# Norms of a hybrid encoder trunk: last squares added on VectorE, sums in one set of matmuls, roots spread by transposes, outputs scaled from PSUM

## Chip, cores and metric

The kernel runs on one core of one Trainium2 chip. The metric is the device time of one execution in microseconds. Before the change the median of three runs is 1268.73 us (1267.92 to 1269.37).

## What is computed

The trunk has two residual layers with a token mixer each (a gated spatial MLP, then RWKV-7) and a gated convolutional feed-forward after each mixer. Every one of the four sub-layers is preceded by an RMS norm, and one norm closes the trunk. The sequence is 512 tokens, the model width 1024, all data float32.

```
def rms_norm(x, g):
    y = xf * lax.rsqrt(jnp.mean(xf * xf, axis=-1, keepdims=True) + RMS_EPS)
    return y * g

h = x
for i in range(DEPTH):                       # DEPTH = 2
    hn = rms_norm(h, norm_mix_g[i])
    h = h + (sgu_mixer if i % 2 == 0 else rwkv7_mixer)(hn, ...)
    h = h + conv_ffn(rms_norm(h, norm_ffn_g[i]), ...)
return rms_norm(h, norm_final_g)
```

## The kernel before

The residual stream `h` is held transposed in SBUF: eight tiles of 128 features by 512 tokens. The stages run in the order gating (`sgu`), feed-forward 0 (`ffn`), RWKV (`rwkv_first`, `rwkv_main`), feed-forward 1, output. Matrix products are made from two parts for each operand, a rounded one and the rest (`split`, L224; `mm3`, L316), so that each fp32 product is three matmuls of a fast type. Weights arrive by DMA, ScalarE casts the high part (L236) and VectorE subtracts to get the low part (L237).

**How a norm is made.** Because the norm's factor is one number for each token, the projections run on `h` times the gain without it, and the factor is applied to their results. When a stage updates tile `k` of `h`, `absorb` (L332) makes the operands of the next projection and squares the tile on ScalarE (L342, L345). GpSimd adds the squares of tiles 0 to 6 into `ss` (L347); those of tile 7 stay apart in `sq`. `rstd` (L349) then

- sums over the 128 features on TensorE: for each of four blocks of 128 tokens one matmul of `ss` and one of `sq` against a column of ones (L355, L356), accumulated in a PSUM column. These are plain fp32 matmuls, outside `mm3`;
- takes the inverse roots: VectorE scales and adds epsilon (L372), GpSimd raises to the power -0.5 (L373). This gives a 128x4 tile with tokens on the partitions;
- spreads the roots to all partitions: for each block a matmul whose stationary operand is the root column broadcast to 128x128 and whose moving operand is the identity (L362), into PSUM tile `z`;
- copies `z` to SBUF as `rb` on ScalarE (L365). Consumers multiply by `rb`.

`rstd` is a generator with two steps, so that callers put projections between sums and spread: one projection in a feed-forward (L533 to L539), the second half of the value projection in the gating stage (L456, L472), and in `rwkv_first` parts of two low-rank projections (L678 to L684): four of the eight tiles of the first ahead of the sums, the other four and two tiles of the second between sums and spread, the rest after.

**The output.** `output` (L584) makes the final norm for one half of the tokens. The last projection of feed-forward 1 is cut into token halves and its pieces are ordered by hand (L561), so that the first half's norm runs while TensorE works on the second half. After a half's last piece VectorE adds it to `h` (L569) and ScalarE squares it (L595). ScalarE has multiplied `h` by the gains into four tiles `o` of two features blocks each (L602). Sums (L606, L607), roots, spread (L613) and the copy to SBUF (L616) follow. The scaling by the spread roots is done tile by tile, 128x256 each: six on VectorE and the pair `k == 4` on GpSimd (L622). SyncE stores each pair (L623). In the second half `wait` (L588) puts matmuls without use into TensorE's order ahead of the sums and ahead of the spread (L591).

The order of instructions on each engine comes from a scheduler at compile time; `issue_after` pins a part of it. Each engine then works through its own list in order, and semaphores hold it where an input isn't there yet.

Of the kernel before, what the change touches and what calls it, by code (L numbers as in the profile page):

```python
# [12 lines left out]
F32 = mybir.dt.float32  # L13
F32R = mybir.dt.float32r
AF = mybir.ActivationFunctionType
ALU = mybir.AluOpType
# [4 lines left out]
P = 128  # L21
# [123 lines left out]
class Emit:  # L145
# [203 lines left out]
    def rstd(self):  # L349

        nc = self.nc
        q = self.acc()
        for b in range(4):
            bs = slice(b * P, (b + 1) * P)
            nc.tensor.matmul(q[:, b:b + 1], self.ss[:, bs], self.c("one", 1), start=True, stop=False)  # L355
            nc.tensor.matmul(q[:, b:b + 1], self.sq[:, bs], self.c("one", 1), start=False, stop=True)  # L356
# [4 lines left out]
        for b in range(4):  # L361
            nc.tensor.matmul(z[:, b * P:(b + 1) * P], r[:, b:b + 1].to_broadcast([P, P]), self.c("ident", P),  # L362
                             start=True, stop=True)
# [48 lines left out]
    def sgu(self, gain):  # L412
        nc, tc, A = self.nc, self.tc, self.A
        with ExitStack() as ctx:
# [24 lines left out]
            for hf in range(2):  # L439
# [15 lines left out]
                if hf == 0:  # L455
                    norm = self.rstd()  # L456
                    r = next(norm)
# [126 lines left out]
    def output(self, hs):  # L584
# [8 lines left out]
        n = T // 2  # L593
        sq = self.gp.tile([P, n], F32, tag="sq", bufs=2, name=self.uid("sq"))
        nc.scalar.activation(sq, self.h[KT - 1][:, hs], AF.Square)  # L595
        yield
        q = self.acc()
# [5 lines left out]
        wait(T)  # L603
        for b in range(2):
            bs = slice(b * P, (b + 1) * P)
            nc.tensor.matmul(q[:, b:b + 1], self.ss[:, hs][:, bs], self.c("one", 1), start=True, stop=False)  # L606
            nc.tensor.matmul(q[:, b:b + 1], sq[:, bs], self.c("one", 1), start=False, stop=True)  # L607
# [4 lines left out]
        for b in range(2):  # L612
            nc.tensor.matmul(z[:, b * P:(b + 1) * P], r[:, b:b + 1].to_broadcast([P, P]), self.c("ident", P),  # L613
                             start=True, stop=True)
        rb = self.gp.tile([P, T], F32, tag="rb", bufs=1, name=self.uid("rb"))[:, 0:n]
        nc.scalar.copy(rb, z)  # L616
        yield
        out = self.out.rearrange("k p t -> p k t")
        for k in (0, 2, 4, 6):
            t = o[k // 2]  # L620
            for i in range(2):
                (nc.gpsimd if k == 4 else nc.vector).tensor_tensor(t[:, i], t[:, i], rb, ALU.mult)  # L622
            nc.sync.dma_start(out[:, k:k + 2, hs], t)  # L623
# [42 lines left out]
    def rwkv_first(self, r, ep):  # L666
# [11 lines left out]
        self.dense(lw[0], self.first, hx[:4], last=False)  # L678
        norm = self.rstd()
        next(norm)  # L680
        self.dense(lw[0], self.first, hx[4:], first=False, c0=4 * P)
        self.dense(lw[1], w, hx[:2], last=False)
# [725 lines left out]
```

## Time and profile before

| | us |
|---|---|
| median of three runs | 1268.73 |
| lowest, highest | 1267.92, 1269.37 |
| the profiled execution's own time | 1264.91 |
| its span in the profile | 1263.1 |
| TensorE busy in it | 1241.9 |
| VectorE, ScalarE, GpSimd busy | 856.1, 629.7, 98.0 |

In the profile, PE is TensorE, PEld its weight loads, DVE VectorE, ACT ScalarE, POOL GpSimd, SP SyncE. A timeline row gives the start in the span, the duration (of a merged group if it ends in x2 or more), the engine, the line, the operation and what it writes and reads; brackets give the engine's idle time just before and what ended it. TensorE's matmuls overlap, so its pace is read from one start to the next, not from the duration. A row of the windows view gives for each engine the busy time and the number of instructions, then TensorE's granted clock as a share of full speed, the DMA engines' share and the bytes moved in GB/s. In the chain of waits a row gives the start, the length and the work on the path that ended last.

### The profile page before, as it was taken

The page shows a single profiled execution, that of the slowest core. Times are in us where ns is not written, and L with a number is a line of the kernel's source. Part 1 is how long each engine was busy: PE and PEld are TensorE (multiplying, and loading weights), DVE is VectorE, ACT ScalarE, POOL GpSimd, SP SyncE. Part 2 cuts the span into 40 slices and gives each one's busy share as a digit, 9 for nine tenths or more (in the row PEclk, how much of TensorE's full clock was granted, in tenths as well). Part 3 has the DMA queues.
Part 4 walks back from the last instruction along what each step waited for, and adds up shares of the span by engine and source line. Part 5 has one row for each costly group of instructions (what it writes and reads, how often), then busy time and mean ns, then how long its engine had stood idle before and what let it go on. Part 6 is the DMA issues. An engine that isn't in the chain of part 4 may idle for free.

```text
span 1263.1 us, 19531 instructions
## 1 busy us (share of the span) xinstructions
PE 1241.9 (98%) x7591; PEld 1007.9 (80%) x7591; DVE 856.1 (68%) x1403; ACT 629.7 (50%) x1082; POOL 98.0 (8%) x121
## 2 busy tenths in 40 slices
PE   9999999999999999999999999899999999999997
PEld 6878888888888888877777776678888888888886
DVE  6466568888886454675789897765677777773233
ACT  6544446556555433475676657423544544443322
POOL 4100200000000010000000022222000000000002
PEclk9999999999999999999999999999999999999998
DMA  7332357777656765325868799764222333333332
GB/s 258 104 100 84 130 167 240 247 252 245 195 166 203 228 215 184 97 91 192 218 200 226 215 244 230 213 171 138 96 95 91 99 100 100 96 88 105 92 92 80
DMA packets 115452, 201.65 MB, mean 160 GB/s; under 512 B 21600, under 2 KB 53600, under 8 KB 115360
## 3 DMA queue, kind: packets, MB, share of 16 engines
q10 hardware_dynamic: 39104, 112.87, 29.3%
q1 hardware_dynamic: 76256, 87.54, 23.2%
q8 instruction: 59, 0.97, 0.3%
q14 instruction: 33, 0.27, 0.1%
HBM read 152.93 MB, written 47.45 MB: 159 GB/s over the span
## 4 chain that ended last, share of the span: by engine, by line
PE 86%; DVE 6%; DMA 1%; issue 1%; ACT 1%; POOL 0%; SPq 0%; DVEq 0%; ACTq 0%; POOLq 0%
PE mm L320 9%; PE mm L322 9%; PE mm L321 9%; PE aux L320 6%; PE aux L322 6%; PE aux L321 6%; PE e L321 6%; PE e L320 6%; PE e L322 6%; PE us L321 5%; PE us L322 5%; PE us L320 5%; PE aux L938 1%; DVE tt L1015 1%; DVE pr L1014 1%; PE aux L952 1%
## 5 line engine op out<-in xcount | busy, mean ns | idle before, releaser
L236 ACT CAST w<-w 128x512 fp32r<-128x512 f32 x340 | 206.5, 611 | 360.8 <-PE e L322 91.1
L237 DVE TENSOR_TENSOR w<-w,w 128x512 fp32r<-128x512 f32 x340 | 232.1, 685 | 184.7 <-ACT w L236 184.4
L320 PE MATMUL mm<-mxh,w 128*128 128x512 f32 x416 | 169.7, 408 | 0.2 <-ACT vt L837 0.2
L321 PE MATMUL mm<-mxl,w 128*128 128x512 f32 x416 | 163.8, 394 | 0.0
L322 PE MATMUL mm<-mxh,w 128*128 128x512 f32 x416 | 163.7, 394 | 0.0
L347 POOL TENSOR_TENSOR ss<-ss,sq 128x512 f32<-128x512 f32 x30 | 40.7, 1355 | 770.7 <-issue 592.9
L320 PEld LDWEIGHTS mm<-mxh,w 128*128 128x128 f32 x416 | 78.1, 188 | 20.1 <-issue 3.3
L322 PEld LDWEIGHTS mm<-mxh,w 128*128 128x128 f32 x416 | 78.2, 188 | 16.7 <-issue 0.7
L321 PEld LDWEIGHTS mm<-mxl,w 128*128 128x128 f32 x416 | 78.2, 188 | 15.5 <-issue 1.3
L545 ACT ACTIVATE cv<-z,par 128x512 f32<-128x512 f32 x88 | 71.7, 817 | 29.4 <-DVE z L543 24.4
L322 PE MATMUL aux<-mxh,w 128*128 128x512 f32 x216 | 84.2, 390 | 0.3 <-DVE w L237 0.3
L320 PE MATMUL aux<-mxh,w 128*128 128x512 f32 x216 | 84.5, 391 | 0.0
L320 PE MATMUL us<-mxh,w 128*128 128x512 f32 x216 | 84.5, 391 | 0.0
L321 PE MATMUL aux<-mxl,w 128*128 128x512 f32 x216 | 84.1, 389 | 0.0
L321 PE MATMUL us<-mxl,w 128*128 128x512 f32 x216 | 84.1, 389 | 0.0
L322 PE MATMUL us<-mxh,w 128*128 128x512 f32 x216 | 84.0, 389 | 0.0
L320 PE MATMUL e<-mxh,w 128*128 128x512 f32 x208 | 81.4, 391 | 0.1
L321 PE MATMUL e<-mxl,w 128*128 128x512 f32 x208 | 81.1, 390 | 0.1
L322 PE MATMUL e<-mxh,w 128*128 128x512 f32 x208 | 80.9, 389 | 0.0
L546 DVE SCALAR_TENSOR_TENSOR cv<-z,par,cv 128x512 f32<-128x512 f32 x88 | 66.1, 752 | 19.9 <-ACT cv L545 19.9
L547 DVE SCALAR_TENSOR_TENSOR cv<-z,par,cv 128x512 f32<-128x512 f32 x88 | 66.0, 752 | 2.9
L322 PEld LDWEIGHTS aux<-mxh,w 128*128 128x128 f32 x216 | 40.5, 188 | 9.2 <-DVE w L237 0.8
(1089 smaller groups left out, 2574.8 us busy)
## 6 DMA issues: line engine op xcount, KB each, us to landing
w<-in_wup ACTq DMA_DIRECT2D x88, 512.0 KB, 3.6
w<-in_wdn ACTq DMA_DIRECT2D x32, 512.0 KB, 3.7
st<-std SPq DMA_DIRECT2D x30, 320.0 KB, 6.2
w<-wkd ACTq DMA_DIRECT2D x16, 512.0 KB, 4.9
w<-wvd ACTq DMA_DIRECT2D x16, 512.0 KB, 5.6
w<-wod ACTq DMA_DIRECT2D x16, 512.0 KB, 4.2
w<-in_wdn ACTq DMA_DIRECT2D x16, 384.0 KB, 3.4
w<-in_wsu ACTq DMA_DIRECT2D x8, 512.0 KB, 3.7
```

The source lines that it names most:

```text
L236: nc.scalar.copy(hi[r, :n], src)
L237: (lo_eng or nc.vector).tensor_tensor(lo[r, :n], src, hi[r, :n].bitcast(F32), ALU.subtract)
L320: mm(acc, wh, xh, start=first, stop=False)
L321: mm(acc, wh, xl, start=False, stop=False)
L322: mm(acc, wl, xh, start=False, stop=last)
L347: nc.gpsimd.tensor_tensor(self.ss, self.ss, self.sq, ALU.add)
L545: nc.scalar.activation(c, z[:, 2:], AF.Identity, scale=cw(2, i), bias=self.p("conv_b", l * 44 + i))
L546: nc.vector.scalar_tensor_tensor(c, z[:, 1:T + 1], cw(1, i), c, ALU.mult, ALU.add)
L547: nc.vector.scalar_tensor_tensor(c, z[:, 0:T], cw(0, i), c, ALU.mult, ALU.add)
L938: nc.tensor.matmul(qs[hd][:, c - ch.start, :], bk[H[hd], c, C * hd:C * hd + P], ar[H[hd], c, :], start=True, stop=True)
L952: nc.tensor.matmul(qs[hd][:, c, :], bk[H[hd], c, C * hd:C * hd + P], dg[H[hd], c, :], start=True, stop=True)
L1014: V.tensor_tensor(q, a, b, ALU.mult)
```

## The change

In `rstd` VectorE adds the last tile's squares to the others' sum, and the sums are one matmul for each block instead of two; the gating stage asks for the old form (`whole=False`). Roots are spread by TensorE transposes of the broadcast column in place of matmuls with the identity. In `output` the first half uses the added form; the second keeps both sources, with the matmuls of `ss` for both blocks put ahead of those of `sq`, and the first useless matmul, now 256 columns wide, between them. The spread roots are no longer copied to SBUF: VectorE multiplies each pair of tiles, 128x2x256, by the PSUM tile broadcast over the pair, and GpSimd takes no part. In `rwkv_first` six tiles of the first low-rank projection stand ahead of the sums, and one tile of the second before the spread.

```diff
+    def spread(self, z, r):
+        for b in range(r.shape[-1]):
+            self.nc.tensor.transpose(z[:, b * P:(b + 1) * P], r[:, b:b + 1].to_broadcast([P, P]), self.c("ident", P))
+
-    def rstd(self):
+    def rstd(self, whole=True):
         nc = self.nc
         q = self.acc()
+        if whole:
+            nc.vector.tensor_tensor(self.ss, self.ss, self.sq, ALU.add)
         for b in range(4):
-            bs = slice(b * P, (b + 1) * P)
-            nc.tensor.matmul(q[:, b:b + 1], self.ss[:, bs], self.c("one", 1), start=True, stop=False)
-            nc.tensor.matmul(q[:, b:b + 1], self.sq[:, bs], self.c("one", 1), start=False, stop=True)
+            for i, x in enumerate((self.ss,) if whole else (self.ss, self.sq)):
+                nc.tensor.matmul(q[:, b:b + 1], x[:, b * P:(b + 1) * P], self.c("one", 1), start=i == 0, stop=i == 1 or whole)
...
-        for b in range(4):
-            nc.tensor.matmul(z[:, b * P:(b + 1) * P], r[:, b:b + 1].to_broadcast([P, P]), self.c("ident", P),
-                             start=True, stop=True)
+        self.spread(z, r)
...
-                    norm = self.rstd()
+                    norm = self.rstd(whole=False)
...
+        whole = hs.start == 0
...
-        wait(T)
-        for b in range(2):
-            bs = slice(b * P, (b + 1) * P)
-            nc.tensor.matmul(q[:, b:b + 1], self.ss[:, hs][:, bs], self.c("one", 1), start=True, stop=False)
-            nc.tensor.matmul(q[:, b:b + 1], sq[:, bs], self.c("one", 1), start=False, stop=True)
+        ss = self.ss[:, hs]
+        q = self.acc()
+        if whole:
+            nc.vector.tensor_tensor(ss, ss, sq, ALU.add)
+            for b in range(2):
+                nc.tensor.matmul(q[:, b:b + 1], ss[:, b * P:(b + 1) * P], self.c("one", 1), start=True, stop=True)
+        else:
+            for x in (ss, sq):
+                for b in range(2):
+                    nc.tensor.matmul(q[:, b:b + 1], x[:, b * P:(b + 1) * P], self.c("one", 1), start=x is ss and b == 0,
+                                     stop=x is sq, skip_group_check=True)
+                if x is ss:
+                    wait(n)
...
-        for b in range(2):
-            nc.tensor.matmul(z[:, b * P:(b + 1) * P], r[:, b:b + 1].to_broadcast([P, P]), self.c("ident", P),
-                             start=True, stop=True)
-        rb = self.gp.tile([P, T], F32, tag="rb", bufs=1, name=self.uid("rb"))[:, 0:n]
-        nc.scalar.copy(rb, z)
+        self.spread(z, r)
...
-        for k in (0, 2, 4, 6):
+        for k in range(0, KT, 2):
             t = o[k // 2]
-            for i in range(2):
-                (nc.gpsimd if k == 4 else nc.vector).tensor_tensor(t[:, i], t[:, i], rb, ALU.mult)
+            nc.vector.tensor_tensor(t, t, z.unsqueeze(1).to_broadcast([P, 2, n]), ALU.mult)
             nc.sync.dma_start(out[:, k:k + 2, hs], t)
...
-        self.dense(lw[0], self.first, hx[:4], last=False)
+        self.dense(lw[0], self.first, hx[:6], last=False)
         norm = self.rstd()
         next(norm)
-        self.dense(lw[0], self.first, hx[4:], first=False, c0=4 * P)
-        self.dense(lw[1], w, hx[:2], last=False)
+        self.dense(lw[0], self.first, hx[6:], first=False, c0=6 * P)
+        self.dense(lw[1], w, hx[:1], last=False)
         rb = next(norm)
-        self.dense(lw[1], w, hx[2:], first=False, c0=2 * P)
+        self.dense(lw[1], w, hx[1:], first=False, c0=P)
```

1 line of the change is left out of this document (removed).

## Prediction

> **What bounds the kernel now.** I read the page first, then TensorE's timeline around each norm, the other engines' timelines beside it, and last the chain of waits and fine windows at the end.
>
> ```profile
> span 1263.1 us, 19531 instructions
> ...
> PE 1241.9 (98%) x7591; PEld 1007.9 (80%) x7591; DVE 856.1 (68%) x1403; ACT 629.7 (50%) x1082; POOL 98.0 (8%) x121
> ...
> PE 86%; DVE 6%; DMA 1%; issue 1%; ACT 1%; POOL 0%; SPq 0%; DVEq 0%; ACTq 0%; POOLq 0%
> ```
>
> TensorE is busy for 98% of the span and makes up 86% of the chain that ended last. One long window, the second feed-forward stage, shows how that holds locally:
>
> ```profile
> 905.00:1230.00 325.00, 325.00 (x1435) 269.12 (x1434) 206.16 (x301) 140.99 (x221) 6.45 (x5) 1.00 0.31 96
> ```
>
> All 325.00 us are TensorE's, at a granted clock of 1.00. A pass that TensorE no longer has to make in such a stage should therefore shorten the kernel by its own length. What remains to be seen is whether each norm lies in such a place. Here is the norm of that stage on TensorE:
>
> ```profile
> 891.83 0.28 PE L355 MATMUL us<-cst,ss 128*128 128x1 f32 x2
> ...
> 893.53 0.48 PE L320 MATMUL mm<-mxh,w 128*128 128x512 f32 x1
> ...
> 899.06 1.05 PE L362 MATMUL aux<-cst,rt 128*128 128x128 f32 x8
> 899.87 0.48 PE L320 MATMUL e<-mxh,w 128*128 128x512 f32 x1
> ```
>
> From 891.83 to 893.53 TensorE does the sums: four blocks, two sources, two passes for each fp32 matmul ("x2" in a row), 16 passes in 1.70 us, 0.106 us each. The 24 projection matmuls up to 899.06 take 5.53 us, 0.23 us each. The spread of the roots is 8 passes in 0.81 us, 0.10 each. Nothing in between waits.
>
> **The change, part by part.** *Sums.* In the norms of both feed-forward stages and of the RWKV stage the sums fall from 16 passes to 8: 8 x 0.106 = 0.85 us each, 2.55 us for three. The gating stage keeps both sources there and gains nothing on this part.
>
> VectorE's new add is 128x512 f32; the nearest row is 0.69 us (L543, below). Is it hidden?
>
> ```profile
> 889.15 0.62 ACT L345 ACTIVATE sq<-h 128x512 f32<-128x512 f32 x1
> 892.02 0.62 ACT L236 CAST w<-w 128x512 fp32r<-128x512 f32 x1 [1.75 <-PE e L322]
> 159.24 0.16 DVE L372 TENSOR_SCALAR rs<-aux 128x4 f32<-128x4 f32 x1 [2.65 <-PE aux L356]
> 518.28 0.16 DVE L372 TENSOR_SCALAR rs<-mm 128x4 f32<-128x4 f32 x1 [2.07 <-PE mm L356]
> 893.70 0.16 DVE L372 TENSOR_SCALAR rs<-us 128x4 f32<-128x4 f32 x1 [2.70 <-PE us L356]
> ```
>
> The bracket is VectorE's idle time ahead of the scale step: 2.65, 2.07 and 2.70 us. In the last case it is free from 891.00, the squares are there at 889.77, so the add ends near 891.7, just before the sums at 891.83. The projection matmuls cover it; without that cover it costs 0.7 us a norm. I take nothing.
>
> *Spread.* Four matmuls of two passes become four transposes. The kernel has transposes of the same shape in its scan:
>
> ```profile
> L1260 PE MATMUL aux<-cst,y x32: 271/273/329, 756.3 to 861.3; 128*128 128x128 f32 x32
> ...
> 756.30 0.66 PE L1260 MATMUL aux<-cst,y 128*128 128x128 f32 x4
> 756.71 0.48 PE L320 MATMUL mm<-mxh,w 128*128 128x512 f32 x1
> ```
>
> Eight calls of four make 32, so a transpose is one pass, and four of them take 0.41 us against 0.81. That is 0.40 us in each of four norms (gating, both feed-forwards, RWKV): 1.60 us.
>
> *The moved work in the RWKV stage.* Six matmuls move ahead of the sums, and the spread comes after nine instead of eighteen. No DMA moves with them.
>
> ```profile
> 516.40 0.28 PE L355 MATMUL mm<-cst,ss 128*128 128x1 f32 x2
> ...
> 518.10 0.48 PE L320 MATMUL e<-mxh,w 128*128 128x512 f32 x1
> ...
> 522.27 1.05 PE L362 MATMUL aux<-cst,rt 128*128 128x128 f32 x8
> ...
> 527.05 0.39 PE L322 MATMUL us<-mxh,w 128*128 128x512 f32 x1
> 527.50 0.50 PE L320 MATMUL e<-mxh,w 128*128 128x512 f32 x1
> ...
> 528.30 0.40 PE L320 MATMUL aux<-mxh,w 128*128 128x512 f32 x1
> 528.77 0.51 PE L321 MATMUL e<-mxl,w 128*128 128x512 f32 x1
> ...
> 518.52 1.40 POOL L373 TENSOR_TENSOR rt<-rs,mhalf 128x4 f32<-128x4 f32 x1 [3.40 <-DVE rs L372]
> ...
> 20.87 3.21 POOL L373 TENSOR_TENSOR rt<-rs,mhalf 128x4 f32<-128x4 f32 x1 [2.56 <-DVE rs L372]
> ```
>
> The roots are done at 519.92, 1.82 us after TensorE left the sums at 518.10. Nine matmuls cover 9 x 0.23 = 2.07, so the spread should still find them ready, with 0.25 us to spare. If GpSimd took 3.21 us, as it did in the first norm, TensorE would wait 1.6 us. The spread comes 0.68 us earlier in TensorE's order (three matmuls fewer in all ahead of it) and 0.85 us earlier for the shorter sums, so the spread factor is there about 1.9 us sooner. After the projections TensorE waits for the mixing chain that starts from this factor: 0.22 us over the pitch at 527.50 and 0.24 at 528.77. Bounds are nothing and both; a chain 1.9 us earlier against projections 1.25 us earlier leaves 0.65 for 0.46, so I take 0.45.
>
> *The end.* The output goes in halves of 256 columns. In the first half TensorE still works on the last projection:
>
> ```profile
> 1245.42 0.28 PE L606 MATMUL aux<-cst,ss 128*128 128x1 f32 x2
> ...
> 1246.22 0.36 PE L320 MATMUL mm<-hid12h,w 128*128 128x256 f32 x1
> ...
> 1247.40 0.71 PE L613 MATMUL e<-cst,rt 128*128 128x128 f32 x4 [0.46 <-POOL rt L373]
> ...
> 1250.94 0.28 PE L322 MATMUL mm<-hid21h,w 128*128 128x256 f32 x1
> ...
> 1251.66 0.41 DVE L569 TENSOR_TENSOR h<-h,mm 128x256 f32<-128x256 f32 x1
> ...
> 1248.55 3.19 DVE o L622 x6
> ```
>
> Eight passes become four (0.80 to 0.40) and four spread passes become two (0.10 each, so 0.20): TensorE ends 0.60 us earlier. The wait for the roots (0.46) I leave as it is; the new add (0.41 by the L569 row) could lengthen the first half by that, or the emptier chain could take the wait away. The residual add L569 starts at 1251.66 although the last matmul ended at 1251.22: it is queued on VectorE behind the six scalings of the first half, which run to 1251.74. Four scalings that start some 0.8 us earlier and need 2.5 to 2.8 us end before it is due. That gives 0.40.
>
> ```profile
> 1255.38 0.38 ACT rb L616
> 1255.78 0.42 DVE o L622
> ...
> 1255.83 1.82 POOL L622 TENSOR_TENSOR o<-o,rb 128x256 f32<-128x256 f32 x2 [1.33 <-ACT rb L616]
> ...
> 1257.68 0.37 SPq L623 DMA_DIRECT2D out_yT<-o  x1
> ...
> SPq L623 <- POOL o L622: 57.3, 2, 52.1
> ...
> 1255.00:1255.50 0.50, 0.27 (x3) 0.07 (x1) 0.00 (x0) 0.12 (x1) 0.00 (x0) 0.98 0.00 0
> ...
> 1258.50:1259.00 0.50, 0.00 (x0) 0.00 (x0) 0.44 (x2) 0.00 (x0) 0.00 (x0) 0.50 0.81 262
> 1261.50:1262.00 0.50, 0.00 (x0) 0.00 (x0) 0.00 (x0) 0.00 (x0) 0.00 (x0) 0.50 0.31 105
> ...
> 166.30 0.69 DVE L543 TENSOR_TENSOR z<-mm,rb 128x512 f32<-128x512 f32 x1 [0.17 <-ACT rb L365]
> ```
>
> In the second half two passes less stand between the last squares and the roots (0.22), two less in the spread (0.20), and the copy to SBUF goes (1255.38 to 1255.78, 0.40). Then comes the part that a count of operations would miss: the first store is issued only at 1257.68, 1.90 us after scaling begins, because SyncE's queue has GpSimd's pair first (it ends at 1257.65). From there on the stores bind: bytes flow from about 1258.6 to 1261.65, four times 256 KB in 3.05 us. Without GpSimd the first pair is ready 0.69 us after scaling begins (L543: a 128x512 product with one PSUM operand), and the store goes out at about 0.74. The other pairs follow every 0.7 us, while one store's bytes take 0.76, so the transfer stays the limit and the end moves by 1.90 - 0.74 = 1.16. If the queue still waited for the last pair, the first store would go out 2.8 us after the start and 0.9 would be lost instead.
>
> A rule of the Trainium skill bears on the removed copy: "VectorE: DVE Perf Modes", Rules for kernel authors, says to take the slower PSUM source as it is, or to copy to SBUF first if many operations read it. By the rows of this case the copy costs 0.40 us, and a 128x512 product from PSUM takes 0.69 us where two 128x256 ones from SBUF take 0.42 each, so four readers are not many here. Following the rule's second half would give back the 0.40.
>
> The sum: 2.55 + 1.60 + 0.45 + 0.60 + 0.40 + 0.22 + 0.20 + 0.40 + 1.16 = 7.6 us. The profiled execution took 1264.91 us (span 1263.1), so it would take 1257.3; the median of the three runs, 1268.73, lies 3.8 us higher, and 1268.7 - 7.6 gives 1261.1.
>
> **The rivals.** *The norm's own chain comes late* (0.14). The add or the roots are queued badly and TensorE waits. If the add stands behind the next weight split, whose cast (892.02) ends at 892.64, split and add end at 894.0 and the sums start 2.2 us late. One such norm leaves 5.4 us: 1263.3. So does the slow GpSimd case, with 1262.7. Three norms would leave 1.0, no change. VectorE's long idle times speak against it.
>
> *The early savings are absorbed* (0.08). In the scan TensorE isn't the only limit. If what the gating, first feed-forward and RWKV norms bring (0.40 + 1.25 + 1.25 + 0.45 = 3.35 us) ended in waits there, 4.2 us would remain: 1264.5. Against it: those waits are for work that starts earlier too.
>
> *The transposes are no single pass* (0.05). Then 1.60 and about 0.4 at the end are lost: 1263.1. The 32 rows of L1260 speak against it.
>
> *The clock falls* (0.05), the case in which it gets slower. The column after the engines in the fine windows is the granted clock: it leaves 1.00 in the window 1255.00 to 1255.50, in which TensorE's last passes lie, and is 0.50 for the 7.5 us that are left. So the clock follows recent work, and the change takes counted passes out of five places. A stretch as long as that one at half clock in the middle costs 3.75 us. Two of them eat the gain, and from three on it is slower: 1272.4 with three. Against it, L1260's transposes run among matmuls with the clock at full. "TensorE: Matmul & The Clock Gate", Part 4, of the Trainium skill says that transposes don't count as work for the clock gate; the scan's transposes show no fall, and each new group lasts only 0.4 us among dense matmuls.
>
> **How the numbers follow.** The forecast has 0.68. A measurement of this kernel can tell about 0.2% (2.5 us) from no change. Faster by more: 0.68, with 0.10 of the late chain, 0.06 of the absorbed savings and 0.05 of the transposes, 0.89. The rest of those, 0.06, is within it, and 0.05 is slower. The low end takes the whole wait for roots in the output (0.46) and the spread of the runs (0.8) on top, with further waits in the mixing chain: 1258.8. The high end, 1265.0, takes in the transposes, the absorbed savings and one or two late norms.
>
> **What would show it.** Right: eight passes of 0.85 us in three norms, spreads of 0.41 us, no gap near 526 us, the residual add within 0.4 us of the last matmul, the first store within 0.8 us of the first scaling, and 3.05 us of bytes after it. Wrong: TensorE idle before the sums or before a transpose, a VectorE add queued behind a weight split, stores still in another order than the scalings, or a clock below 1.00 ahead of the end.

## The result and the profile after

The kernel after took 1258.41 us (median of four executions, 1257.85 to 1258.64), the kernel before 1269.05 us beside it (four, 1267.92 to 1271.46): a ratio of 0.9919, interval 0.9897 to 0.9941. The gain is 10.6 us where the prediction summed 7.6, and 1258.4 lies 0.4 us below the predicted range. The profiled execution after took 1258.64 us. From its page:

```profile
span 1256.8 us, 19427 instructions
...
PE 1238.0 (98%) x7543; PEld 1003.2 (80%) x7543; DVE 856.3 (68%) x1403; ACT 627.7 (50%) x1080; POOL 95.0 (8%) x117
...
PE 86%; DVE 7%; issue 1%; POOL 1%; ACT 0%; DMA 0%; DVEq 0%; POOLq 0%; ACTq 0%
```

TensorE still bounds the kernel with 98% of the span. But the two profiled spans differ by 1263.1 - 1256.8 = 6.3 us only, so most of the distance between 6.3 and 10.6 is not in these two traces. First the places of the change. The second feed-forward norm on TensorE's timeline:

```profile
889.77 0.95 PE L362 MATMUL us<-cst,ss 128*128 128x1 f32 x8
890.58 0.48 PE L320 MATMUL mm<-mxh,w 128*128 128x512 f32 x1
...
896.11 0.60 PE L352 MATMUL aux<-cst,rt 128*128 128x128 f32 x4
896.47 0.48 PE L320 MATMUL e<-mxh,w 128*128 128x512 f32 x1
```

The sums take 0.81 us (1.70 before), the spread 0.36 us (0.81). VectorE's new add is done 1.2 us before the sums begin:

```profile
887.90 0.69 DVE L359 TENSOR_TENSOR ss<-ss,sq 128x512 f32<-128x512 f32 x1
```

In the gating stage the shorter spread buys almost nothing. TensorE's waits between 53 and 157 us for the v tiles, before and after (engine, tile and line, what it waited for: us in total, times, longest):

```profile
PE e L495 <- DVE vt L469: 0.2, 1, 0.2
```

```profile
PE e L499 <- DVE vt L473: 0.6, 1, 0.6
```

VectorE's four products of the v tiles depend on the roots, not on the spread; they end when they ended, and TensorE waits for the last of them by what it saved. In the RWKV stage the roots cause no wait, but the pause after the projections stays (0.37 us between the last projection matmul at 523.51 and the first mixing matmul, a pitch being 0.23):

```profile
518.51 0.60 PE L352 MATMUL aux<-cst,rt 128*128 128x128 f32 x4
518.87 0.48 PE L320 MATMUL us<-mxh,w 128*128 128x512 f32 x1
...
523.88 0.50 PE L320 MATMUL e<-mxh,w 128*128 128x512 f32 x1
...
525.10 0.50 PE L321 MATMUL e<-mxl,w 128*128 128x512 f32 x1
```

The end: TensorE's timeline, then VectorE's, then SyncE's first store of the second half, then what SyncE's queue waited for.

```profile
1242.29 0.61 PE L612 MATMUL aux<-cst,ss 128*128 128x1 f32 x4
...
1243.93 0.43 PE L352 MATMUL e<-cst,rt 128*128 128x128 f32 x2 [0.45 <-POOL rt L377]
...
1247.20 0.28 PE L322 MATMUL mm<-hid21h,w 128*128 128x256 f32 x1
```

```profile
1247.52 0.42 DVE L573 TENSOR_TENSOR h<-h,mm 128x256 f32<-128x256 f32 x1 [0.63 <-PE mm L322]
...
1250.67 2.48 DVE L629 TENSOR_TENSOR o<-o,e 128x512 f32<-128x512 f32 x4 [1.36 <-PE e L352]
```

```profile
1251.39 0.37 SPq L630 DMA_DIRECT2D out_yT<-o  x1
```

```profile
SPq L630 <- DVE o L629: 414.9, 4, 410.6
```

The residual add now follows its matmul (VectorE was free for 0.63 us before it). The first store goes out 0.72 us after the first scaling, against 1.90, and SyncE's queue waits for VectorE, no longer for GpSimd. Before the first half's sums TensorE stands still for 0.28 us: the last matmul started at 1241.89, a pitch is 0.12, the sums start at 1242.29, because the add ends at 1242.23.

A landmark is the start of the same instruction in both traces. The gains between landmarks, before minus after:

| from, to | gain there, us |
|---|---|
| start to the gating stage's spread (weights and first loads, nothing changed) | 0.76 |
| gating spread, with its later wait | 0.07 |
| first feed-forward: sums 0.89, spread 0.46 | 1.35 |
| RWKV: sums, spread, move, to the first mixing matmul | 1.44 |
| from there to the second feed-forward sums (nothing changed) | -1.56 |
| second feed-forward: sums 0.89, spread 0.45 | 1.34 |
| output: TensorE 0.33, residual add 0.40, chain to the first scaling 0.97, stores 1.15 | 2.85 |

That makes 6.3 us; the change's own places alone make 7.1. The -1.56 comes from a stretch that the change doesn't touch, shown here by windows of the kernel after (from, to and length, busy us of PE, PEld, DVE, ACT and POOL with their counts, then the granted clock, DMA share, GB/s):

```profile
680.00:681.00 1.00, 1.00 (x8) 0.80 (x7) 1.00 (x4) 0.88 (x2) 0.00 (x0) 1.00 0.28 98
681.00:682.00 1.00, 1.00 (x4) 0.79 (x3) 1.00 (x2) 0.41 (x2) 0.00 (x0) 0.59 0.22 47
...
683.00:684.00 1.00, 1.00 (x6) 0.91 (x5) 0.96 (x5) 1.00 (x3) 0.00 (x0) 0.50 1.04 323
684.00:685.00 1.00, 1.00 (x7) 1.00 (x7) 1.00 (x4) 0.06 (x1) 0.00 (x0) 0.71 0.86 261
685.00:686.00 1.00, 1.00 (x11) 0.59 (x10) 0.91 (x2) 0.97 (x3) 0.00 (x0) 1.00 0.01 2
```

For 3.4 us the clock is 0.50 in the middle of the kernel, and matmuls start every 0.43 us instead of every 0.23. TensorE is "busy" all the while: only the clock's column shows it. The profiled execution before has no such stretch ahead of its end.

### The profile page after: what moved, and what is told of

Its sections match the earlier page's. It is cut to its first block, busy times and chain, and to the rows that moved or that the text cites. A ratio compares the mean times of both kernels' runs of the same rounds, so it can differ in the third digit from the quotient of the medians.

```text
span 1256.8 us, 19427 instructions
## 1 busy us (share of the span) xinstructions
PE 1238.0 (98%) x7543; PEld 1003.2 (80%) x7543; DVE 856.3 (68%) x1403; ACT 627.7 (50%) x1080; POOL 95.0 (8%) x117
## 4 chain that ended last, share of the span: by engine, by line
PE 86%; DVE 7%; issue 1%; POOL 1%; ACT 0%; DMA 0%; DVEq 0%; POOLq 0%; ACTq 0%
PE mm L320 9%; PE mm L322 9%; PE mm L321 9%; PE aux L320 6%; PE aux L322 6%; PE aux L321 6%; PE e L320 6%; PE e L321 6%; PE us L320 6%; PE e L322 6%; PE us L322 6%; PE us L321 6%; DVE tt L1022 1%; PE aux L945 1%; DVE pr L1021 1%
## 5 line engine op out<-in xcount | busy, mean ns | idle before, releaser
L237 DVE TENSOR_TENSOR pwl<-pw,pwh 128x512 fp32r<-128x512 f32 (+1 forms) x51 | 34.8, 682 | 19.8 <-DMA wkd<-pwl 4.6
```

The costliest lines, as they stand in the source:

```text
L237: (lo_eng or nc.vector).tensor_tensor(lo[r, :n], src, hi[r, :n].bitcast(F32), ALU.subtract)
```

## The experiments

Two theories. *A, the clock:* the parts are worth about what the prediction summed, and the rest of the gain is half-clock stretches that differ from execution to execution and cost the kernel before more. *B, a part worth more:* some part brings more than was priced. Later a third question came up, what the moved matmuls do. Parts are judged by landmarks in the traces, times by all executions with their mean clock.

**Both kernels again, and each half of the change** (e1 before; e2 after with the output function of before, here its core; e3 before with the output function of after; e4 after).

```
-            nc.vector.tensor_tensor(t, t, z.unsqueeze(1).to_broadcast([P, 2, n]), ALU.mult)
+            for i in range(2):
+                (nc.gpsimd if k == 4 else nc.vector).tensor_tensor(t[:, i], t[:, i], rb, ALU.mult)
```

> The kernel before, unchanged, to see where its executions differ from each other: its profiled one took 1264.91 us, its timed ones 1267.92 to 1271.46. Theory A (clock): the slower ones hold one or more stretches of about 3.4 us at half the granted clock in the scan, worth up to 1.7 us each, as the changed kernel's trace shows one at 681 to 684.5; then this trace, if it lies near 1268 or above, shows two or more windows with a granted clock of 0.50 ahead of the end, and the time above 1264.9 is about 1.7 us for each. Theory B (memory): the clock is 1.00 throughout and the extra 3 to 6 us lie in waits for DMA in the RWKV stage. Ratio 1.000 in either case.

> Everything of the change but the output: sums, transposes and the moved matmuls in the norms ahead of the four sub-layers; the output as before. By the landmarks of the two traces this part brings 0.46 in each of four spreads, 0.89 in each of three sums, less about 0.5 lost to a different order in the gating stage: 4.0 us, ratio 0.9968. If the excess of the measured gain (10.6) over that of the traces (6.3) belongs to the norms, it brings 7 to 8 us, ratio 0.994.

> Only the output changed, the norms as before. By the two traces' landmarks (the first half's last matmul 3.41 us earlier, the span's end 6.3 us earlier) this part brings 2.9 us, ratio 0.9977; by the prediction's terms 3.0. If the excess belongs to the output it brings 6 to 7 us, ratio 0.995. The first store is issued within 0.8 us of the first scaling and bytes flow for 3.05 us after it.

> The changed kernel, unchanged, beside the others on one chip: ratio 0.992. Theory A: the number of half-clock stretches ahead of the end differs from execution to execution and with it the time, 1.6 us for one. Theory B: no such stretch, the same time within 0.5 us. If norms and output are independent its gain is the sum of the two parts' gains within 1 us.

e1: 1268.91 us (1266.40 to 1274.14, 12 executions). e2: 1262.10 (1258.77 to 1264.38, 6). e3: 1266.40 (1261.68 to 1269.42, 12). e4: 1257.69 (1257.14 to 1258.60, 5). Ratios: 1.0006 [0.9992, 1.0021], 0.9947 [0.9930, 0.9964], 0.9979 [0.9964, 0.9993], 0.9917 [0.9903, 0.9930]. By medians the norms bring 6.8 us, more than their landmarks (4.2 us in the table above), the output 2.5 (2.9). The two together make 9.3, 1.9 less than the 11.2 of the whole change in e4, where independent parts were expected to agree within 1 us: medians of these executions don't settle the parts. In their own profiles the halves have the landmarks' amounts, 4.2 us in the places of e2's norms and 2.9 from the second feed-forward sums to the end of e3. The profiled execution of the unchanged kernel before took 1270.42 us this time, 5.5 more than the one shown ahead of the prediction, and its windows say why:

```profile
726.00:727.00 1.00, 1.00 (x38) 0.89 (x36) 1.00 (x1) 0.63 (x2) 0.00 (x0) 0.96 0.73 236
727.00:728.00 1.00, 1.00 (x6) 0.78 (x8) 0.86 (x3) 0.99 (x3) 0.00 (x0) 0.50 0.04 13
728.00:730.00 2.00, 2.00 (x38) 1.94 (x38) 1.76 (x8) 0.49 (x1) 0.00 (x0) 0.50 0.73 231
```

It runs at half clock from 726.9 to 733.7, and also from 20.4 to 23.8 and from 791.8 to 795.2 us. Of the 5.5 us, landmarks place 1.2 between the first norm's sums and the gating spread and 4.5 from 583 us, in the RWKV stage, to the second feed-forward sums, where these stretches lie. So theory A has its mechanism in the kernel before. One length comes back in all these traces, 3.4 us or two to four times it, and the places are few: near 20, 606, 682, 722 to 735 and 779 to 795 us.

**The spreads alone** (e7: output and sums as before).

```
-            nc.tensor.matmul(z[..b..], r[:, b:b + 1].to_broadcast([P, P]), self.c("ident", P), ...)
+            self.nc.tensor.transpose(z[..b..], r[:, b:b + 1].to_broadcast([P, P]), self.c("ident", P))
```

> The kernel before with only the spreads of the four norms made by transposes; sums, their place in the RWKV stage and the output as before. By the parts: each spread is one pass per block, 0.35 to 0.41 us instead of 0.81, so 0.40 to 0.46 us each and 1.6 to 1.8 us in all, read from the start of the same matmul after each norm. If transposes gave the clock gate less work, half-clock windows should appear behind the norms (near 53, 165, 523 and 899 us). Undisturbed time 1264.9 - 1.7 = 1263.2; with the clock dips of the kernel before its executions lie between that and 1270, and the median at about 1267. If instead the median of the kernel after is low because transposes are worth more than their length, this kernel should come out at 1264 or less in the median with its landmarks no further ahead than 1.8 us.

1267.36 us (1264.71 to 1269.93, 12 executions), ratio 0.9992 [0.9978, 1.0006]: no gain. Each spread is 0.45 us shorter, but in the RWKV stage the work behind it comes late: TensorE's waits between 516 and 546 us, and ScalarE's order there.

```profile
PE e L320 <- ACT mxh L236: 1.7, 2, 1.2
```

```profile
525.35 1.33 ACT L661 ACTIVATE mt<-h,par 128x512 f32<-128x512 f32 x2
527.54 0.62 ACT L236 CAST w<-w 128x512 fp32r<-128x512 f32 x1 [0.85 <-PE us L322]
528.06 1.13 ACT L236 CAST mxh<-mt 128x512 fp32r<-128x512 f32 x2
```

In the kernel before the first cast of a mixed tile stood ahead of that weight cast:

```profile
525.28 1.34 ACT L657 ACTIVATE mt<-h,par 128x512 f32<-128x512 f32 x2
526.82 0.62 ACT L236 CAST mxh<-mt 128x512 fp32r<-128x512 f32 x1 [0.20 <-DVE mt L658]
527.48 0.62 ACT L236 CAST w<-w 128x512 fp32r<-128x512 f32 x1
```

The order is fixed at compile time, and the shorter spread turned it round: now the weight cast, which waits 0.85 us for TensorE to leave its slot, holds the cast that TensorE will wait for. Between 506 and 540 us this kernel loses 0.9 us on the kernel before, which eats what the feed-forward spreads bring (0.46 each).

**One set of sums and the move, spreads by matmuls** (e8).

```
-            self.nc.tensor.transpose(z[..b..], r[:, b:b + 1].to_broadcast([P, P]), self.c("ident", P))
+            self.nc.tensor.matmul(z[..b..], r[:, b:b + 1].to_broadcast([P, P]), self.c("ident", P), ...)
```

> The kernel before with only one set of sums on TensorE (VectorE's add) in three norms and the work moved in the RWKV stage; spreads by matmuls and the output as before. By the parts: 8 passes less in each of three norms, 0.85 to 0.89 us each, less 0.4 us that the changed compile-time order costs in the gating stage if that belongs to this part, 2.1 to 2.7 us at the first matmul behind the second feed-forward stage's sums. In the RWKV stage the spread of two passes takes the 0.2 us that the roots had to spare, so no wait for the roots of more than 0.1 us. Undisturbed time 1264.9 - 2.4 = 1262.5; with the clock dips the median lies at about 1266 to 1267. If one set of sums is worth more than its passes, this median is 1264 or less with landmarks no further ahead than 2.7 us.

1264.84 us (1262.46 to 1270.06, 12 executions), ratio 0.9978 [0.9962, 0.9993]. On TensorE's timeline:

```profile
894.48 0.95 PE L363 MATMUL us<-cst,ss 128*128 128x1 f32 x8
895.29 0.48 PE L320 MATMUL mm<-mxh,w 128*128 128x512 f32 x1
```

0.81 us again; against the kernel before 0.92 us are gained in the first feed-forward norm, 0.88 in the RWKV stage, with no wait there, and 0.89 in the second. The 0.4 us that I had put down to a changed order in the gating stage are not lost here (103.19 us from the gating spread to the sums, 103.22 before; 103.61 with transposes): they belong to the spread, as its wait for v shows. So 2.7 us in the trace, 2.8 by the medians, no extra.

**The move alone undone** (e9, and e13 for its profile).

```
-        self.dense(lw[0], self.first, hx[:6], last=False)
+        self.dense(lw[0], self.first, hx[:4], last=False)
...
-        self.dense(lw[1], w, hx[:1], last=False)
+        self.dense(lw[1], w, hx[:2], last=False)
```

> The kernel after without the moved work in the RWKV stage: the sums stand after four tiles and the spread after six tiles of the low-rank projections again, as in the kernel before; all else as after. By the prediction the move is worth at most the 0.45 us of the gaps behind the projections: the first mixing matmul of the RWKV stage then comes 0.45 us later than in the kernel after, counted from the first feed-forward stage's norm, and the times differ by less than 1 us. By the theory that came from the run with transposes alone (there TensorE waited 1.23 us and again 0.45 us for the mixing chain, because a weight cast that waits for TensorE stands ahead of the mixed tile's cast on ScalarE), the move is what lets the shorter norm pay at all: without it the waits for mixed tiles between 523 and 540 us add up to 1 us or more, most of the 1.3 us that sums and spread save there.

> The kernel after without the moved work in the RWKV stage, once more for a profile. If the move is worth 0.45 us at most (the prediction), the first mixing matmul comes no more than 0.5 us later than in the kernel after, counted from the start of the first feed-forward stage's sums (367.35 us in the kernel after), and TensorE's waits for mixed tiles behind it are below 0.3 us in sum. If the move is what lets the shorter norm pay, that distance is longer by 1 us or more, or the waits that follow up to 540 us make up as much.

e9: 1258.64 us in the median of five executions (1258.44 to 1262.07); the sixth, the profiled one, took 3422 us with matmuls starting every 0.84 us instead of every 0.23, and nothing is read from it. e13: 1257.86 us, one execution without any half-clock stretch ahead of its end. Its trace has the wait of the spreads alone again:

```profile
PE e L320 <- ACT mxh L236: 1.6, 2, 1.2
```

At 505 us it lies 0.45 us behind the kernel after, at 537 us 2.01 us: without the move 1.56 us are lost there. The times don't show it: on one chip e9's five executions have a median of 1258.64 us and the kernel after 1259.03 (e10, below).

**The move with the spreads** (e14: e7 with the move).

> The kernel with transposes alone, with the moved work of the RWKV stage added (two sets of sums stay, and the output is that of the kernel before). If the order on ScalarE was the cause of the waits of 1.23 and 0.45 us, both are gone here, since the casts of the first two mixed tiles now stand ahead of the weight cast: the sum of TensorE's waits for mixed tiles between 520 and 545 us falls from about 1.7 to below 0.3 us, and at 540 us this kernel stands about 1.4 us ahead of the one with transposes alone, counted from the first feed-forward stage's sums. If instead the chain from the roots to the mixed tiles is simply too long for the shorter spread, the waits stay at 1 us or more.

1262.71 us (1262.24 to 1263.99, 5 executions), ratio 0.9954 [0.9937, 0.9971]. TensorE waits for no mixed tile; from 507 to 540 us it gains 1.38 us on e7. On ScalarE the weight cast is out of the way early and both mixed tiles come with the next cast:

```profile
522.35 1.39 ACT L661 ACTIVATE mt<-h,par 128x512 f32<-128x512 f32 x2 [0.82 <-DVE h L713]
523.65 0.61 ACT L236 CAST w<-w 128x512 fp32r<-128x512 f32 x1
525.01 1.28 ACT L236 CAST mxh<-mt 128x512 fp32r<-128x512 f32 x2 [0.75 <-DVE mt L662]
```

So the move is worth about 1.4 to 1.6 us in the RWKV stage beside a shorter norm, through the order on ScalarE, and not by closing the pause behind the projections, which stays.

**The output's parts.** e6 takes GpSimd out of the scalings of the kernel before; e5 puts the copy to SBUF back into the kernel after.

```
-                (nc.gpsimd if k == 4 else nc.vector).tensor_tensor(t[:, i], t[:, i], rb, ALU.mult)
+                nc.vector.tensor_tensor(t[:, i], t[:, i], rb, ALU.mult)
```

```
         self.spread(z, r)
+        rb = self.gp.tile([P, T], F32, tag="rb", ...)[:, 0:n]
+        nc.scalar.copy(rb, z)
+        z = rb
```

> The kernel before, with the third pair of the output's scalings on VectorE too instead of GpSimd. If the first store waited for GpSimd's pair (the prediction's reading of 1.90 us from the first scaling to the first store), it now goes out 0.84 to 0.9 us after the first scaling (two scalings of 0.42 us), the bytes still take 3.05 us, and the end comes 1.0 to 1.1 us sooner counted from the first scaling of the second half. If the queue waits for something else (the last of the eight scalings), the first store goes out about 3.3 us after the first scaling and the end comes 1.4 us later. In the first half VectorE has eight scalings instead of six, so the residual add there is held 0.8 us longer than before, which gives most of the gain back: the timed median should differ from the kernel before by less than 1 us, which the clock dips of single executions hide.

> The kernel after with one thing put back: ScalarE copies the spread factor of the output to SBUF, and VectorE scales the pairs of tiles from there. Priced by parts (the sum of the prediction): the copy adds 0.38 to 0.40 us between the second half's spread and the first scaling; scaling a pair from SBUF keeps about 0.6 to 0.7 us, so the first store goes out about 0.7 us after the first scaling as in the kernel after, and the span's end moves by 0.4 us: 1258.1 where the kernel after gave 1257.7. If instead reading PSUM is what makes the pair slow, a pair from SBUF takes well under 0.6 us and the copy pays for itself: no change. Theory of the clock dips: everything ahead of the end is the kernel after's own program, so its executions should be as close together as that kernel's (within 1.5 us) if their closeness belongs to the program, and should scatter over 4 to 6 us, as those with the old output did, if it was chance.

e6: 1266.18 us (1263.84 to 1271.96, 12 executions), ratio 0.9983 [0.9969, 0.9998]. Its timeline at the first half's scalings and around the first store of the second half, and its queue's waits:

```profile
1251.21 2.77 DVE L622 TENSOR_TENSOR o<-o,rb 128x256 f32<-128x256 f32 x8 [1.99 <-ACT rb L616]
...
1258.04 1.76 DVE L622 TENSOR_TENSOR o<-o,rb 128x256 f32<-128x256 f32 x5 [2.10 <-ACT rb L616]
1258.83 0.37 SPq L623 DMA_DIRECT2D out_yT<-o  x1
```

```profile
SPq L623 <- DVE o L622: 56.5, 7, 51.1
```

The first store goes out 0.79 us after the first scaling, and from that scaling to the span's end it is 6.20 us instead of 7.33: GpSimd's pair was worth 1.13 us there, where the prediction has 1.16. The expectation for the first half failed: the residual add comes not 0.8 us later but 0.39 us sooner, counted from the first scaling (2.72 us against 3.11). VectorE's eight scalings take 2.77 us together, where six took 3.19 in the kernel before: two of those six, the ones that ran beside GpSimd's, took 0.96 us each, all others 0.41 to 0.43. From the first half's sums to the end e6 gains 1.53 us, and by the medians 1.5 (1267.66 before on that chip), not less than 1 as expected.

e5: 1259.98 us (1257.24 to 1262.67, 6 executions), ratio 0.9926 [0.9906, 0.9945]. The first scalings and the first store of its second half:

```profile
1252.30 1.89 DVE L632 TENSOR_TENSOR o<-o,rb 128x512 f32<-128x512 f32 x3 [1.82 <-ACT rb L626]
1253.01 0.37 SPq L633 DMA_DIRECT2D out_yT<-o  x1
```

From the residual add to the first scaling it takes 3.61 us instead of 3.15, so the copy costs 0.46; the scatter of the executions hides it in the time. A pair from SBUF takes 0.63 us, from PSUM 0.62. The Trainium skill ("VectorE: DVE Perf Modes", Rules for kernel authors) offers both ways, the PSUM source as it is or a copy first for many readers; with these fp32 pairs the trace shows nothing that a copy could win back.

**What brings the half clock** (e11: the kernel after with three runs of needless work in the dense second feed-forward stage).

```
+        for i in range({1: 37, 3: 76, 5: 384}[m]):
+            with self.tc.issue_after(self.last(mybir.EngineType.PE)):
+                if m == 1:
+                    self.nc.tensor.matmul(z[:, 0:P], ident, ident, start=True, stop=True)
+                elif m == 3:
+                    self.nc.tensor.transpose(z[:, 0:P], ident, ident)
+                else:
+                    self.nc.tensor.matmul(z[0:32, 0:32], ident[0:32, 0:32], ident[0:32, 0:32], start=True, stop=True)
```

> The kernel after with three runs of needless TensorE work inside the dense second feed-forward stage, whose clock is 1.00 throughout in every run so far: 37 plain fp32 128x128 matmuls (two passes each, about 7.5 us), then 15 to 30 us later 76 transposes of 128x128 (one pass each, about 7.6 us), then 384 matmuls of 32x32 (8 us or more). Each lasts longer than two of the 3.4 us windows in which the clock was seen to change, so each holds a whole window. Theory of the dips (the clock falls for a window after one in which TensorE did little counted work): the 32x32 run is followed by 3.4 us or more at 0.50. By the clock page of the Trainium skill transposes are not counted: then a fall to 0.50 sits in or right behind the transposes too, 3 to 7 us after their start, and none behind the plain matmuls. If transposes count as the plain matmuls do, both or neither fall. If no run of the three brings a fall, the dips come from something other than the kind of TensorE's work.

1316.27 us (one execution; the added work is 8.2, 8.2 and 39.2 us long). Windows in the plain matmuls, the transposes, and the 32x32 matmuls, which begin at 1226.9 and end near 1266.0 us:

```profile
1156.00:1158.00 2.00, 2.00 (x20) 2.00 (x20) 0.00 (x0) 0.00 (x0) 0.00 (x0) 1.00 0.00 0
...
1196.00:1198.00 2.00, 2.00 (x15) 1.82 (x14) 0.00 (x0) 0.00 (x0) 0.00 (x0) 1.00 0.00 0
...
1227.00:1229.00 2.00, 2.00 (x66) 2.00 (x67) 0.69 (x1) 0.62 (x1) 0.00 (x0) 1.00 0.00 0
1229.50:1230.00 0.50, 0.50 (x18) 0.50 (x16) 0.00 (x0) 0.00 (x0) 0.00 (x0) 0.79 0.70 123
...
1269.00:1270.00 1.00, 1.00 (x3) 0.78 (x3) 0.00 (x0) 0.00 (x0) 0.00 (x0) 0.50 0.00 0
1271.00:1272.00 1.00, 1.00 (x6) 0.79 (x5) 0.07 (x1) 0.62 (x1) 0.00 (x0) 1.00 0.00 0
```

The clock stays at 1.00 in and behind the plain fp32 matmuls and the transposes. In the 32x32 matmuls it falls about 3 us after their start, though TensorE counts as fully busy, stays at 0.50, and comes back between 1270 and 1271 us, more than 4 us after dense matmuls resume. The scan's matmuls of 64 and 32 columns are of this kind, and so are the sums of a norm, which move one column: in e1 the clock falls at 20.4 us, right behind the first norm's sums (18.24 to 20.05 us), in e10 at 605.4 us, behind 64-column matmuls from 603.2 to 605.0 us. Each such group is there in every execution, and the fall in some; the sums of the other norms, 1.70 us or less, brought none in any trace.

What the falls have in common shows when the 15 traces other than e9's are laid side by side. In each of them every change of the clock lies a whole number of 3.413 us after its first rise, and that rise comes at 4.3 to 7.1 us, differently in each execution. Cut along this grid up to 1240 us, the traces hold 20 falls, and each follows a window whose matmuls moved at most 3584 columns together. A dense window moves 7680, and of the nearly 5,400 other windows at full clock only 25 moved so few. So the place of the grid, which differs between executions, decides how much of a group of narrow matmuls lies in one window: near 20 us falls follow windows of 1035 to 3088 columns, none follows one of 3597 or more, and between 2575 and 3086 both occur. The windows that plain matmuls or transposes filled in e11 held 3840 to 3968 columns, just above. That few columns bring the fall is read from these traces; made on purpose it was only in e11.

The rule of the Trainium skill that transposes do not count as work for the clock gate ("TensorE: Matmul & The Clock Gate", Part 4) does not show here: in the one execution of e11, 8.2 us of them left the clock alone, as the prediction's argument against that rival had it.

**The kernel after on one more chip, and a step beyond it** (e10 after unchanged; e12 asks for the output's first half two tiles later, six matmuls of cover ahead of its sums).

```
-                    for hf, k0, kn in ((0, 0, 8), (1, 0, 8), (0, 8, 8), (0, 16, 6), (1, 8, 4), (1, 12, 4), (1, 16, 6)):
+                    for hf, k0, kn in ((0, 0, 8), (1, 0, 8), (0, 8, 8), (0, 16, 6), (1, 8, 6), (1, 14, 2), (1, 16, 6)):
-                        if k0 == 12:
+                        if k0 == 14:
```

> The kernel after, unchanged, on one more chip. If its nine executions so far lay close together (1257.1 to 1258.6) by chance, these scatter over 3 us or more like those of the kernel with the copy kept (1257.2 to 1262.7), and the median of all lies near 1259. If the closeness is the program's own, all of them lie between 1257 and 1259. In both cases, at equal mean clock (0.997) it stands 7 to 8 us below the kernel before, which is the sum of the prediction.

> The kernel after with the output's first half asked for two projection tiles later, so that six matmuls of 256 columns (0.72 us) stand between the last squares and the sums in place of none. In the kernel after TensorE idles 0.28 us there for VectorE's add and 0.45 us for the roots. The sums now find the add done: 0.28 us less, the wait for the roots stays at 0.45 us; the first half's scalings end 0.5 us later, still before the residual add, so the end comes 0.2 to 0.3 us sooner counted from the last matmul of the first half's tile. If the scalings hold the residual add, nothing is gained. In the time that can't be told from the kernel after; its executions add to those that show whether the kernel after scatters.

e10: 1259.03 us (1257.11 to 1260.76, 6 executions), ratio 0.9925 [0.9910, 0.9941]: the closeness of the first nine executions was partly chance. e12 on the same chip: 1258.37 us (1256.05 to 1259.67, 6), ratio 0.9921 [0.9907, 0.9936]. Its trace:

```profile
1242.81 0.50 PE L612 MATMUL aux<-cst,ss 128*128 128x1 f32 x4
...
1244.35 0.43 PE L352 MATMUL e<-cst,rt 128*128 128x128 f32 x2 [0.46 <-POOL rt L377]
...
1246.88 0.28 PE L322 MATMUL mm<-hid21h,w 128*128 128x256 f32 x1
```

The sums no longer wait, the wait for the roots stays. From the last matmul of the first half's tile (1240.53) to this last one it is 6.35 us instead of 6.75, and the first scaling of the second half (1250.36) comes 0.39 us sooner by the same count. In the trace it beats both kernels; in the time it can't be told from the kernel after.

**All executions together.** Mean clock is that of a whole execution, averaged over the executions; "at 0.997" is a fit of one slope for all kernels (1.04 us for each 0.001 of mean clock). The executions of the kernel before are the 83 beside the experiments, e1 among them; those of the first session have no clock on record.

| kernel | executions | lowest | median | mean clock | at 0.997 |
|---|---|---|---|---|---|
| before | 83 | 1264.64 | 1267.98 | 0.9941 | 1265.5 |
| after | 15 | 1257.11 | 1258.40 | 0.9961 | 1257.5 |
| norms only (e2) | 6 | 1258.77 | 1262.10 | 0.9950 | 1259.6 |
| output only (e3) | 12 | 1261.68 | 1266.40 | 0.9950 | 1263.9 |
| spreads only (e7) | 12 | 1264.71 | 1267.36 | 0.9946 | 1264.7 |
| sums and move (e8) | 12 | 1262.46 | 1264.84 | 0.9938 | 1262.2 |
| no move (e9, e13) | 6 | 1257.86 | 1258.55 | 0.9973 | 1259.5 |

The kernel before at 0.997 took 1264.64 to 1264.90 us (4 executions), at 0.995 1266.03 to 1269.43 (27), at 0.990 1272.08 to 1274.14 (3). The kernel after at 0.997 took 1257.11 to 1257.85 (5), and at 0.998 no less, 1257.69 to 1258.64 (3). The medians of the two groups at 0.997, 1264.76 and 1257.54, differ by 7.2 us, and the landmarks gave 7.1.

That agreement is luck in part, because mean clock also counts the half clock behind the last matmuls. It fills 4.6 to 7.6 us of the span in the seven profiles with the old output and 2.2 to 5.0 us in the seven with the new one (6.1 and 3.8 in the mean). At equal mean clock the kernel after therefore holds more half clock where it costs time: 2.3 us of it, 0.0009 of mean clock, or some 0.9 us by the slope. At equal stretches the executions would differ by 8 to 9 us, and 1 to 2 us of that have no place in the landmarks.

The scan, the recurrence in the RWKV stage, is left alone by the change and has waits that vary as much. The profiled execution after and e4's ran the same program. After a stretch at 20 us e4 is 1.39 us behind until 779 us, and level at 790 us. One matmul's wait in each, the kernel after first, then e4, makes up 0.8 us of it:

```profile
781.20 0.51 PE L1214 MATMUL us<-vu,st 128*64 128x64 f32 x10 [1.35 <-issue]
```

```profile
781.75 0.51 PE L1214 MATMUL us<-vu,st 128*64 128x64 f32 x10 [0.54 <-issue]
```

The clock is 1.00 in both. The same wait is 1.25 us in e10, 0.21 in e12 and absent in e13. So time lost or won ahead of the scan can vanish in it; what the wait is for, the traces don't say.

## Why the prediction was wrong, and where it was right

The step that failed is the last of the sum: "the median of the three runs, 1268.73, lies 3.8 us higher, and 1268.7 - 7.6 gives 1261.1". It takes what lies between an execution and the median as a constant that the kernel after would keep, and puts the spread of the runs at 0.8 us. The runs showed a loss that changes from execution to execution. The profiled execution before, with no half-clock stretch ahead of its end, is near the fastest of its kernel (1264.64); 83 others have a median of 1267.98, 3.3 us above the fastest, and the one profiled again in e1 paid 5.5 us more, in the places of its stretches. The kernel after pays less: its 15 executions have a median of 1258.40, 1.3 us above their fastest. So the medians differ by 9.6 us, and by 10.6 in the first session's four each, where the sum had 7.6 and the landmarks have 7.1. Working from the profiled execution alone, 1264.91 - 7.6 = 1257.3, the prediction's own intermediate number, lies within the five executions of the kernel after at 0.997, though these may hold a stretch themselves.

Where the 9.6 us come from is known in part. The change's own places make 7.1. Half-clock stretches make some 1.2 by an estimate: mean clock without the end's part (6.1 and 3.8 us) leaves 2.6 stretches of 3.4 us in a usual execution of the kernel before and 1.8 in one of the kernel after, at 1.56 us each, the cost measured in the kernel after. The rest, some 1.3 us, stays open; the scan's waits are large enough for it.

For theory B, a part worth more than its price, the places of the change leave nothing: landmarks give the whole change 7.1 us and the halves 4.2 and 2.9, and the profiles of e2 and e3 agree. By the fit the norms bring 5.9 us and the output 1.6, so 1.7 too much and 1.3 too little. That half-clock stretches cost this time is shown (the halved pace in the windows, and the time that follows the mean clock), and also that a run of 32x32 matmuls brings one. Why the kernel after meets fewer, or whether 15 executions only had luck, is not: e7 and e14 differ by six moved matmuls and the order that comes with them, and their mean clocks were 0.992 to 0.997 and 0.996 to 0.998. With 5 to 15 executions of each I can't say which place decides.

The terms of the sum, predicted and measured:

- *Sums:* 0.85 each, measured 0.89, and VectorE's add hidden in all three norms. Right.
- *Spreads:* 0.40 each, measured 0.45 in both feed-forward norms, but 0.07 in the gating stage: the saving became a wait for VectorE's v products. This is the rival of absorbed savings; the waits near 781 us are a second place where it can act.
- *RWKV:* 0.85 + 0.40 + 0.45 = 1.70, measured 1.44. The reason given for the 0.45 was wrong: the pause stays. What the move does is keep the mixing chain in order on ScalarE; alone the spread there costs 0.9 us, and the prediction saw nothing of it since it read TensorE's path and GpSimd's, and not ScalarE's.
- *Output, first half:* TensorE 0.60, measured 0.33, the difference being the 0.28 us for the add that the text named as possible; residual add 0.40, measured 0.40, but the reason given, four scalings in place of six, is not the only one: in e6 eight scalings free it 0.39 us sooner, since GpSimd's pair had held VectorE up.
- *Output, second half:* 0.82 to the first scaling, measured 0.97; stores 1.16, measured 1.15, and GpSimd's pair was the cause (1.13 in e6).
- *Rivals:* late norms, no single pass: none seen. "The clock falls" had the right mechanism on the wrong side. It asked whether the change would bring half-clock stretches; they were there already, though not in the one profile at hand.

## What to carry to other kernels

When the profiled execution lies several us below the median, find out what the median pays before a sum is subtracted from it: compare the mean clock of executions, less the part that the end has, and look for windows below 1.00. A saving on TensorE counts only where what comes next is ready: ask for each place which queue, ScalarE's among them, holds the next operand, because a shorter step can reorder it for the worse. Where medians scatter by several us, judge parts by the distance between the same two instructions in two traces.

## What the hardware showed unexpectedly

The granted clock halves inside a kernel whose TensorE is 98% busy, for about 3.4 us or a multiple (681.2 to 684.6 us in the kernel after, 726.9 to 733.7 in e1), and such a stretch costs about half its length where TensorE binds: the one of 3.4 us cost 1.56 us. A run of 32x32 matmuls brings it after about 3 us, while 8.2 us of fp32 128x128 matmuls or of transposes do not. In 15 traces its changes lie on a grid of 3.413 us whose place differs between executions, and all 20 falls follow windows in which the matmuls moved 3584 columns or fewer.

A 128x256 product on VectorE takes 0.42 us alone and 0.94 to 0.96 us beside the same product on GpSimd (L622 in the kernel before, against e6).
